# A decoder trunk whose sixteen head pairs each get an ending of their own: parts or whole product last, and another token order in the next matmuls

## The chip, the core and the metric

The kernel runs on one core of one Trainium2 chip. The metric is device time in microseconds (us) of one execution; the time before is the median of three runs, 2437.17 us (2436.08 to 2437.2). Lower is better.

## What is computed

A causal decoder trunk of two layers over 256 tokens with 2048 features, 16 heads of 128, and a gated MLP of 5632. Cut to what matters:

```python
for i in range(DEPTH):                      # DEPTH = 2
    a = rmsnorm(h, attn_norm[i])
    if i % 2 == 0:   # 8 stick-breaking heads, then 8 dilated-window heads
        h = h + sb_dilated_mixer(a, positions, w_in_even[i // 2], w_out_even[i // 2])
    else:            # 16 forgetting-attention heads
        h = h + fox_mixer(a, w_in_odd[i // 2], b_forget[i // 2], w_out_odd[i // 2])
    h = h + conv_ffn(rmsnorm(h, ffn_norm[i]), w_up[i], conv_w[i], conv_b[i], w_down[i])
    gate = jax.nn.sigmoid(rmsnorm(h, ple_norm[i]) @ w_ple_gate[i])
    h = h + gate * (p[i] @ w_ple[i])
return rmsnorm(h, final_norm)
```

Every head computes scores from q and k, a weighting of them, and the product of these weights with v.

## The kernel before, in words

Activations lie feature by token (128 partitions by 256 tokens). Each operand of a projection is split into a high part, rounded to the matmul type F32R, and a low part, the rest; a product is three matmuls, `PARTS = ((0, 0), (0, 1), (1, 0))`: high by high, high by low, low by high. Weights are streamed by DMA (`issue_group`, L160) and split by ScalarE and VectorE (L176, L177) into a ring of four tiles `w`. Almost all of TensorE's work is of one shape: a stationary 128x128 tile and 256 moving columns. `gemm_unit` (L222 to L232) issues 24 such matmuls for four blocks of the contraction, `gemm_v` (L258 to L267) the same with the roles of weight and activation exchanged, and each such unit ends with one `tick`. Tile names: `psq`, `psk`, `psv` are the projections to q, k and v, `psp` the per-layer embedding, `pso` the projection out of the mixer, `psu`, `psd`, `psg` the MLP up, down and the gate.

Two heads are worked on at a time. Pair number = 8 times the layer + the pair in its layer: pairs 0 to 3 are stick-breaking, 4 to 7 dilated, 8 to 15 forgetting heads. A pair's attention is put into the stream of projection matmuls as three short pieces, by `defer(n, fn)`, which runs `fn` after n more ticks, so that VectorE and ScalarE have the time of some units for the softmax:

- the scores (`sb_first` L467 or `sm_first` L511, tile `scs`): per head one product of whole float32 operands q and k (128x128), and three matmuls of parts with 256 columns. In `sm_first` the whole product stands ahead of the parts; forgetting heads have a third product ahead of both (L518);
- the second piece: for stick-breaking pairs the suffix sums (`sb_second` L492, F32R throughout), for the others six float32 transposes (`sm_second` L553, L559), tile `sps`;
- the product with the values (`attend` L575, tile `avp`): per head one whole float32 product (L580) and three of parts (L583), the whole one ahead.

So in a trace every piece ends either with **parts last** (F32R) or with **float32 last**, and the projection goes on behind it. All is one in-order stream on TensorE; nothing but the program's order decides what stands there.

Behind every piece `shake()` sets a count of two. The next two matmuls of `gemm_unit` or `gemm_v` then go through their 256 tokens (in `gemm_v` columns) in another order, on the moving side and in PSUM alike, so that the result is the same:

```python
def walk(ap):
    return ap.rearrange("p (a b c) -> p b a c", a=2, c=8)
```

Eight tokens of the first half, eight of the second, and so on. This is called a walk of side 8 over two matmuls, (8, 2), below. Three more shakes stand outside the pairs: five and eight ticks after the start of the first layer's projections, and behind the forget gates at the start of the second layer. Other pieces on TensorE have no shake behind them: the sums of a norm (`norm_sums` L321, tile `nps`), its rows (`norm_rows` L337, `rps`), both float32, and the running sums of the forget gates (`cps`, L612 to L620, float32).

Of the kernel before, what the change touches and what calls it, by code (L numbers as in the profile page):

```python
# [17 lines left out]
P = 128  # L18
D = 2048
S = 256  # L20
# [80 lines left out]
GROUPS = _groups(UNITS)  # L101


@with_exitstack
def trunk(ctx: ExitStack, tc: tile.TileContext, xT, pT, pos, gains, conv, bf, cst, wst, out):
    nc = tc.nc
# [30 lines left out]
    def at_tile(name):  # L137
        return psum.tile([P, 2, 512], F32, name=name, tag="at", bufs=2)
# [6 lines left out]


    raws, ready = [], []
    at = {"group": 0, "off": 0, "unit": 0, "tick": 0, "rows": 0, "shake": 0}

    def issue_group():  # L150
        g = GROUPS[at["group"]]
# [42 lines left out]
    def defer(n, fn):  # L194
        later.append((at["tick"] + n, fn))
# [10 lines left out]
    PARTS = ((0, 0), (0, 1), (1, 0))  # L206
# [1 line left out]


    def walk(ap):  # L210
        return ap.rearrange("p (a b c) -> p b a c", a=2, c=8)

    def shake():
        at["shake"] = 2

    def walks(*aps):
        if not at["shake"]:
# [290 lines left out]

    SEG = ((0, 128), (128, 384))

    def sm_first(q, k, prepared, fox):  # L511
        full, one = prepared
        sc = at_tile("scs")
        for j in range(2):
            if fox is not None:
                c2, sel, cq, h0 = fox
                lh = sel[:, h0 + j:h0 + j + 1].to_broadcast([P, P])
                nc.tensor.matmul(sc[:, j, 0:384], lhsT=lh, rhs=c2, start=True, stop=False,  # L518
                                 skip_group_check=True)
            nc.tensor.matmul(sc[:, j, 0:128], lhsT=q[:, j, 0:128], rhs=k[:, j, 0:128],  # L520
                             start=fox is None, stop=True, skip_group_check=True)
            for n, (a, b) in enumerate(PARTS):
                nc.tensor.matmul(sc[:, j, 128:384], lhsT=one[a][:, j, :], rhs=full[b][:, j, :],  # L523
                                 start=False, stop=n == 2, skip_group_check=True)
        shake()
        s, pe = t3_tile("s", (P, 2, 384)), t3_tile("pe", (P, 2, 384))
        if fox is None:
            msk = ct[:, C_MDL:C_MDL + 384].unsqueeze(1).to_broadcast([P, 2, 384])
            nc.vector.tensor_add(out=s, in0=sc[:, :, :384], in1=msk)
        else:  # L530
            for j in range(2):
                for t, (a, b) in enumerate(SEG):
                    nc.vector.scalar_tensor_tensor(
                        out=s[:, j, a:b], in0=sc[:, j, a:b], scalar=cq[:, t, h0 + j:h0 + j + 1],
                        in1=ct[:, C_MFX + a:C_MFX + b], op0=ALU.add, op1=ALU.add)
        mx = work.tile([P, 2, 2], F32, name="mx", tag="mx", bufs=2)
        sm = work.tile([P, 2, 2], F32, name="sm", tag="sm", bufs=2)
        rsm = work.tile([P, 2, 2], F32, name="rsm", tag="rsm", bufs=2)
        for t, (a, b) in enumerate(SEG):
            nc.vector.tensor_reduce(out=mx[:, t, :], in_=s[:, :, a:b], axis=AX.X, op=ALU.max,  # L540
                                    negate=True)
        for j in range(2):
            for t, (a, b) in enumerate(SEG):
                nc.scalar.activation(out=pe[:, j, a:b], in_=s[:, j, a:b], func=AF.Exp,
                                     bias=mx[:, t, j:j + 1], accum_out=sm[:, t, j:j + 1])
        nc.vector.reciprocal(out=rsm, in_=sm)
        for t, (a, b) in enumerate(SEG):
            for j in range(2):
                nc.vector.tensor_scalar_mul(out=pe[:, j, a:b], in0=pe[:, j, a:b],
                                            scalar1=rsm[:, t, j:j + 1])  # L550
        return pe, s

    def sm_second(pe, s):  # L553

        sp = at_tile("sps")
        for j in range(2):
            for i in range(3):
                o = sp[:, 0, j * S + i * P:j * S + (i + 1) * P] if i < 2 else sp[:, 1, j * P:(j + 1) * P]
                nc.tensor.transpose(out=o, in_=pe[:, j, i * P:(i + 1) * P], identity=ident)  # L559
        shake()  # L560
        w = in_parts(sp[:, 0, :].rearrange("p (j s) -> p j s", j=2), "w")
        w1 = s.rearrange("p a b -> p (a b)")[:, 0:256]
        nc.scalar.copy(out=w1, in_=sp[:, 1, 0:256])
        return w, w1
# [7 lines left out]
        else:  # L572
            nc.scalar.activation(out=v[1], in_=ps, func=AF.Copy, scale=rT[:, 1:2])

    def attend(hp, w, v, dst):  # L575
        w, w1 = w
        av = at_tile("avp")
        for j in range(2):
            js = slice(j * P, (j + 1) * P)
            nc.tensor.matmul(av[:, 0, j * S + 128:(j + 1) * S], lhsT=v[1][:, js], rhs=w1[:, j * P:(j + 1) * P],  # L580
                             start=j == 0, stop=False, skip_group_check=True)
            for n, (a, b) in enumerate(PARTS):
                nc.tensor.matmul(av[:, 0, j * S:(j + 1) * S], lhsT=v[0][:, a, js], rhs=w[b][:, j, :],  # L583
                                 start=False, stop=n == 2, skip_group_check=True)
        shake()
        parts(dst[:, 2 * hp:2 * hp + 2], av[:, 0, :].rearrange("p (j s) -> p j s", j=2))


# [42 lines left out]
    def head_pair(l, hp, act, dst, st):  # L631
        q = work.tile([P, 2, S], F32, name="q", tag="qkv", bufs=2)
        k = work.tile([P, 2, S], F32, name="k", tag="qkv", bufs=2)
        v = (work.tile([P, 2, S], F32R, name="vp", tag="vp"), work.tile([P, S], F32, name="v", tag="v"))
        full = _cuts(KT)
        if l % 2 == 1 and hp == 0:
            ps = at_tile("psv")
            gemm_vf(ps, act, l)
            for t in range(2):
                values(v, t, ps[:, t, 0:S])  # L640
            st["fox"] = forget_gates(l, ps)
            shake()
        ps = mm_tile("psq")
        gemm(ps, act, "w_in", l, hp * 256, full)
        with_rows(lambda ps=ps: nc.vector.tensor_mul(out=q, in0=ps, in1=rq2))
        ps = mm_tile("psk")
        gemm(ps, act, "w_in", l, D + hp * 256, full)
        with_rows(lambda ps=ps: nc.vector.tensor_mul(out=k, in0=ps, in1=rb2))
        late = max(0, at["rows"] - at["tick"])

        def first():
            if l % 2 == 0 and hp < 4:
                a = sb_first(q, k, st["parts"])
                defer(5, lambda: second(lambda: sb_second(*a)))
            else:
                a = sm_first(q, k, st["parts"], st["fox"] + (2 * hp,) if l % 2 == 1 else None)
                defer(4, lambda: second(lambda: sm_second(*a)))

        def second(fn):
            w = fn()  # L660
            defer(2, lambda: attend(hp, w, v, dst))

        if l % 2 == 0 and hp >= 4:
            rope(q)
            rope(k)

        def prepare():

            if l % 2 == 0 and hp < 4:
                st["parts"] = in_parts(q, "f"), tile_parts(k[:, :, 0:128])  # L670
            else:
                st["parts"] = in_parts(k, "f"), tile_parts(q[:, :, 128:256])

        with_rows(prepare)

        defer(late + (2 + (l % 2 == 0 and hp >= 4) if hp == 7 or (l % 2 == 1 and hp == 0) else 4), first)
        if l % 2 == 1 and hp == 0:
            return
        ps = mm_tile("psv")
        gemm_v(ps, act, l, 2 * D + hp * 256)  # L680
        for i in range(2):
            values(v, i, ps[:, i, :])
# [29 lines left out]
    for l in range(DEPTH):  # L712
        st = {}
        if l == 0:
            split_unit()
            rest_of_start()

            for op in range(8):
                if op in (3, 5, 7):
                    norm_parts(op // 2 - 1, 0, X, tc.keep_in_program_order)  # L720
                ple_up(0, op)
            norm_parts(3, 0, X, tc.keep_in_program_order)
            for i in range(4, 8):
                defer(1 + (i > 5), lambda i=i: norm_parts(i, 0, X, tc.keep_in_program_order))
            constants()
            for i in range(8):
                defer(3 + i, lambda i=i: norm_squares(i, tc.keep_in_program_order))
            norm_finish(True, 12, 14)
            for n in (5, 8):
                defer(n, shake)  # L730
        for hp in range(NH // 2):
            head_pair(l, hp, X, Y, st)
            if l > 0:
# [34 lines left out]
        for op in range(8):  # L768
# [21 lines left out]
            else:  # L790
                more = []
                for j in range(2):
                    for k in range(KT):
                        for n, (a, b) in enumerate(((0, 0), (0, 1), (1, 0))):
                            nc.tensor.matmul(ps[j],  # L795
                                             lhsT=ws[k // 4][:, k % 4, a, j * P:(j + 1) * P],
                                             rhs=X[:, k, b, :], start=k == 0 and n == 0,
# [99 lines left out]
```

## Time and profile before

| | |
|---|---|
| median of three runs | 2437.17 us |
| the profiled execution, its own time | 2434.39 us |
| its span (first to last instruction) | 2432.2 us |
| TensorE matmuls (PE) | 2416.6 us busy, 99%, 21056 records |
| TensorE weight loads (PEld) | 2414.8 us busy, 99% |
| VectorE, ScalarE | 1613.5 us (66%), 1246.2 us (51%) |
| granted TensorE clock | 0.998 |
| TensorE's idle time that a wait explains | 7.1 us in four waits |

A span of PE is pipelined, so "busy" does not say how fast matmuls follow each other. That is read from the chain of waits: a row there gives a start, a duration and a count (`x96`), and duration by count is the time from one matmul to the next. A float32 matmul is recorded as two (`x4` for two instructions).

### The profile page before, as it was taken

What the parts mean: (1) busy time and instruction counts of PE and PEld (TensorE: products, weight loads), DVE (VectorE), ACT (ScalarE), POOL (GpSimd) and SP (SyncE); (2) the same over time, 40 slices, a digit from 0 to 9 for tenths busy, and PEclk for the clock granted to TensorE, in tenths of its full rate; (3) what the DMA queues carried; (4) which work ended last, traced back from release to release, by engine and by line L of the source; (5) the groups of instructions that cost most, each with busy time, mean ns of one, the idle gap of its engine ahead of it and who ended that gap; (6) DMA issues with size and microseconds to landing.
All of it is one profiled execution on the core that took longest, in us unless ns stands there. A gap on an engine that the chain in (4) does not pass through costs nothing.

```text
span 2432.2 us, 48172 instructions
## 1 busy us (share of the span) xinstructions
PE 2416.6 (99%) x21056; PEld 2414.8 (99%) x21056; DVE 1613.5 (66%) x2130; ACT 1246.2 (51%) x1594; POOL 5.9 (0%) x13
## 2 busy tenths in 40 slices
PE   9999999999999999999999999999999999999998
PEld 9999999999999999999999999999999999999997
DVE  7767766776567657767766565666765766577666
ACT  6654455554355445555554454555543554455554
POOL 0000000000000000000000000000000000000000
PEclk9999999999999999999999999999999999999999
DMA  7444455555555555555555454555555555555553
GB/s 281 164 179 167 172 181 183 193 196 198 193 191 192 187 205 197 192 182 204 178 186 176 170 176 160 192 189 191 193 197 197 193 191 185 200 198 194 183 204 122
DMA packets 66818, 458.05 MB, mean 188 GB/s; under 512 B 7552, under 2 KB 7840, under 8 KB 16944
## 3 DMA queue, kind: packets, MB, share of 16 engines
q1 hardware_dynamic: 66576, 454.93, 52.5%
q8 instruction: 164, 2.69, 0.4%
q14 instruction: 46, 0.38, 0.0%
q0 software_dynamic: 32, 0.06, 0.0%
HBM read 452.86 MB, written 2.10 MB: 187 GB/s over the span
## 4 chain that ended last, share of the span: by engine, by line
PE 98%; DMA 1%; DVE 1%; SPq 0%; issue 0%; ACT 0%; POOLq 0%; DVEq 0%
PE psu L232 39%; PE psd L232 20%; PE pso L232 7%; PE psk L232 7%; PE psv L267 7%; PE psq L232 7%; PE psg L232 7%; PE psv L280 0%; PE avp L583 0%; PE psp L232 0%; PE pse L795 0%; DMA h<-in_x 0%; PE scs L523 0%; DMA cv<-in_conv 0%; PE sps L559 0%; PE avp L580 0%
## 5 line engine op out<-in xcount | busy, mean ns | idle before, releaser
L177 DVE TENSOR_TENSOR w<-wr,w 128x1024 fp32r<-128x1024 f32 (+2 forms) x874 | 1046.2, 1197 | 664.7 <-ACT w L176 662.6
L176 ACT CAST w<-wr 128x1024 fp32r<-128x1024 f32 (+2 forms) x874 | 900.6, 1031 | 1041.0 <-PE psu L232 355.0
L232 PE MATMUL psu<-act,w 128*128 128x256 f32 x8448 | 960.3, 276 | 0.0
L232 PEld LDWEIGHTS psu<-act,w 128*128 128x128 f32 x8448 | 959.0, 188 | 0.1
L232 PE MATMUL psd<-act,w 128*128 128x256 f32 x4224 | 479.7, 276 | 0.0
L232 PEld LDWEIGHTS psd<-act,w 128*128 128x128 f32 x4224 | 479.2, 188 | 0.0
L232 PE MATMUL psq<-act,w 128*128 128x256 f32 x1536 | 182.7, 279 | 2.8 <-DVE act L301 2.8
L232 PE MATMUL psk<-act,w 128*128 128x256 f32 x1536 | 184.5, 280 | 0.0
L232 PEld LDWEIGHTS psq<-act,w 128*128 128x128 f32 x1536 | 179.1, 188 | 3.3 <-DVE act L301 3.0
L232 PEld LDWEIGHTS psk<-act,w 128*128 128x128 f32 x1536 | 181.3, 189 | 0.1
L232 PE MATMUL pso<-act,w 128*128 128x256 f32 x1536 | 181.3, 281 | 0.0
L232 PEld LDWEIGHTS pso<-act,w 128*128 128x128 f32 x1536 | 180.6, 189 | 0.0
L267 PE MATMUL psv<-w,act 128*128 128x256 f32 x1440 | 172.3, 279 | 0.0
L267 PEld LDWEIGHTS psv<-w,act 128*128 128x128 f32 x1440 | 170.7, 188 | 0.0
L232 PE MATMUL psg<-act,w 128*128 128x256 f32 x1440 | 164.8, 276 | 0.0
L232 PEld LDWEIGHTS psg<-act,w 128*128 128x128 f32 x1440 | 163.9, 188 | 0.1
L691 DVE TENSOR_TENSOR u<-psu,rb 128x512 f32<-128x512 f32 x88 | 60.8, 691 | 33.0 <-PE psu L232 32.8
L697 DVE SCALAR_TENSOR_TENSOR yv<-u,cv,yv 128x256 f32<-128x256 f32 x176 | 73.3, 477 | 0.0
L697 DVE SCALAR_TENSOR_TENSOR yg<-u,cv,yg 128x256 f32<-128x256 f32 x176 | 73.3, 477 | 0.0
L694 ACT ACTIVATE yg<-u,cv 128x256 f32<-128x256 f32 x88 | 48.1, 593 | 1.1 <-DVE u L691 1.1
L694 ACT ACTIVATE yv<-u,cv 128x256 f32<-128x256 f32 x88 | 48.0, 593 | 0.0
L291 ACT CAST act<-yg 128x512 fp32r<-128x512 f32 x44 | 27.4, 622 | 39.3 <-DVE yg L707 39.3
(182 smaller groups left out, 969.7 us busy)
## 6 DMA issues: line engine op xcount, KB each, us to landing
wr<-in_w SPq DMA_DIRECT2D x388, 1024.0 KB, 4.8
wr<-in_w SPq DMA_DIRECT2D x36, 768.0 KB, 4.3
wr<-in_w SPq DMA_DIRECT2D x8, 896.0 KB, 4.6
h<-in_x SPq DMA_DIRECT2D x4, 512.0 KB, 8.5
wr<-in_w SPq DMA_DIRECT2D x4, 512.0 KB, 10.2
out_dram<-h SPq DMA_DIRECT2D x7, 256.0 KB, 2.5
wr<-in_w SPq DMA_DIRECT2D x2, 816.0 KB, 4.4
pl<-in_w SPq DMA_DIRECT2D x3, 512.0 KB, 7.1
```

Of the source, the lines that this page charges most:

```text
L176: nc.scalar.copy(out=w[:, :, 0, :], in_=raw)
L177: nc.vector.tensor_sub(out=w[:, :, 1, :], in0=raw, in1=w[:, :, 0, :].bitcast(F32))
L232: nc.tensor.matmul(to, lhsT=w[:, k, s, j * P:(j + 1) * P], rhs=rows, start=first and i == 0, stop=last and k == kc - 1 and n == 2, skip_gr ...
L267: nc.tensor.matmul(to, lhsT=act[:, 4 * i + k, a, tsl], rhs=cols, start=i + t + k + n == 0, stop=i == 3 and k == kc - 1 and n == 2, skip_gr ...
L291: nc.scalar.copy(out=dst[:, :, 0, :], in_=src)
L691: nc.vector.tensor_mul(out=u[:, :, 2:], in0=ps, in1=rb2)
L694: nc.scalar.activation(out=y[:, j, :], in_=u[:, j, 2:], func=AF.Identity, bias=cv[:, l, t, 3:4], scale=cv[:, l, t, 2:3])
L697: nc.vector.scalar_tensor_tensor(out=y[:, j, :], in0=u[:, j, tap:tap + S], scalar=cv[:, l, t, tap:tap + 1], in1=y[:, j, :], op0=ALU.mult, ...
```

## The change

Nothing but the order inside three kinds of pieces and the walks behind them changes. On VectorE, ScalarE, GpSimd and SyncE the order of instructions is the same as before, and TensorE executes the same number of matmuls of the same shapes.

`walk` takes its side from a variable, and `shake` takes a way (side, count), with (0, 0), no walk, where none is given. So the ends of `sb_first` and `sb_second` and the place behind the forget gates, whose `shake()` is untouched, now have no walk. `sm_first` and `attend` take a kind, "p" for parts last (as before) or "w" for the whole float32 product last. The tables `SCORES`, `TURNS` and `VALUES` give each pair its ways:

| pair | scores | transposes | product with v |
|---|---|---|---|
| 0 | no walk | no walk | w (8, 2) |
| 1 | no walk | no walk | w, no walk |
| 2 | no walk | no walk | p (4, 1) |
| 3 | no walk | no walk | w (16, 2) |
| 4 | w, no walk | (8, 2) | p (8, 1) |
| 5 | w (8, 1) | (8, 1) | w (4, 1) |
| 6 | w (8, 2) | (4, 1) | w (4, 2) |
| 7 | p (4, 1) | (16, 2) | p (16, 1) |
| 8 | w (16, 2) | (8, 2) | w, no walk |
| 9 | p (16, 2) | (8, 2) | w (8, 1) |
| 10 | p (4, 1) | (8, 1) | w (8, 2) |
| 11 | p (4, 2) | (8, 1) | w (16, 2) |
| 12 | p (32, 2) | (16, 2) | p (16, 2) |
| 13 | w, no walk | (4, 1) | p (4, 1) |
| 14 | w (8, 1) | (4, 2) | p (4, 2) |
| 15 | w (8, 2) | no walk | p (32, 2) |

(For pairs 0 to 3 "transposes" stands for the suffix sums.) Of the two shakes at the start one is left, (4, 1).

```diff
+WAYS = (("w", 0, 0), ("w", 8, 1), ("w", 8, 2), ("w", 16, 2), ("p", 16, 2), ("p", 4, 1), ("p", 4, 2), ("p", 32, 2))
...
     def walk(ap):
-        return ap.rearrange("p (a b c) -> p b a c", a=2, c=8)
-
-    def shake():
-        at["shake"] = 2
+        return ap.rearrange("p (a b c) -> p b a c", a=2, c=at["side"])
+
+    def shake(way=(0, 0)):
+        at["side"], at["shake"] = way
...
+            if kind == "p":
+                whole()
             for n, (a, b) in enumerate(PARTS):
                 nc.tensor.matmul(sc[:, j, 128:384], lhsT=one[a][:, j, :], rhs=full[b][:, j, :],
-                                 start=False, stop=n == 2, skip_group_check=True)
-        shake()
+                                 start=fox is None and kind == "w" and n == 0, stop=n == 2, skip_group_check=True)
+            if kind == "w":
+                whole()
+        shake(way)
...
-        shake()
+        shake(TURNS[pair])
...
+            todo = [(av[:, 0, j * S + 128:(j + 1) * S], v[1][:, js], w1[:, j * P:(j + 1) * P])]
+            inp = [(av[:, 0, j * S:(j + 1) * S], v[0][:, a, js], w[b][:, j, :]) for a, b in PARTS]
+            todo = todo + inp if kind == "p" else inp + todo
+            for n, (o, x, y) in enumerate(todo):
+                nc.tensor.matmul(o, lhsT=x, rhs=y, start=j + n == 0, stop=n == 3, skip_group_check=True)
+        shake(way)
...
-            for n in (5, 8):
-                defer(n, shake)
+            defer(5, lambda: shake((4, 1)))
```

Three places show what this does to TensorE's stream. First the product with the values of pair 9 and the projection behind it, before (`s,v` is the whole product, `wh` and `wl` are the parts; a size written `128x16x2x8` is a walk of side 8):

```order
L580 MATMUL avp<-s,v 128x128
L583 MATMUL avp<-wh,vp 128x256
L583 MATMUL avp<-wl,vp 128x256
L583 MATMUL avp<-wh,vp 128x256
L580 MATMUL avp<-s,v 128x128
L583 MATMUL avp<-wh,vp 128x256
L583 MATMUL avp<-wl,vp 128x256
L583 MATMUL avp<-wh,vp 128x256
L232 MATMUL psk<-act_71,w 128x16x2x8 x2
L232 MATMUL psk<-act_71,w 128x256 x70
```

and after the change:

```order
L604 MATMUL avp<-wh,vp 128x256
L604 MATMUL avp<-wl,vp 128x256
L604 MATMUL avp<-wh,vp 128x256
L604 MATMUL avp<-s,v 128x128
L604 MATMUL avp<-wh,vp 128x256
L604 MATMUL avp<-wl,vp 128x256
L604 MATMUL avp<-wh,vp 128x256
L604 MATMUL avp<-s,v 128x128
L243 MATMUL psk<-act_71,w 128x16x2x8
L243 MATMUL psk<-act_71,w 128x256 x71
```

The float32 product has moved to the end of each head, and one matmul walks where two did. Second, the same piece of pair 7, the last of its layer, with the long projection behind it; before, from its second head on:

```order
L580 MATMUL avp<-s,v 128x128
L583 MATMUL avp<-wh,vp 128x256
L583 MATMUL avp<-wl,vp 128x256
L583 MATMUL avp<-wh,vp 128x256
L232 MATMUL pso<-act_71,w 128x16x2x8 x2
L232 MATMUL pso<-act_71,w 128x256 x646
```

and after:

```order
L604 MATMUL avp<-s,v 128x128
L604 MATMUL avp<-wh,vp 128x256
L604 MATMUL avp<-wl,vp 128x256
L604 MATMUL avp<-wh,vp 128x256
L243 MATMUL pso<-act_71,w 128x8x2x16
L243 MATMUL pso<-act_71,w 128x256 x647
```

Here the order stays, and one walk of side 16 takes the place of two of side 8. Third, the end of the scores of stick-breaking pair 2, before:

```order
L475 MATMUL scs<-fl,xp 128x256
L475 MATMUL scs<-fh,xp 128x256 x2
L475 MATMUL scs<-fl,xp 128x256
L475 MATMUL scs<-fh,xp 128x256
L232 MATMUL psq<-act_70,w 128x16x2x8 x2
L232 MATMUL psq<-act_70,w 128x256 x94
```

and after:

```order
L486 MATMUL scs<-fl,xp 128x256
L486 MATMUL scs<-fh,xp 128x256 x2
L486 MATMUL scs<-fl,xp 128x256
L486 MATMUL scs<-fh,xp 128x256
L243 MATMUL psq<-act_70,w 128x256 x96
```

The walk is gone, and the projection's first 96 matmuls are all plain.

More of the change, by code (lines that the diff above doesn't have):

```diff
@@ L101 @@
 GROUPS = _groups(UNITS)
+WAYS = (("w", 0, 0), ("w", 8, 1), ("w", 8, 2), ("w", 16, 2), ("p", 16, 2), ("p", 4, 1), ("p", 4, 2), ("p", 32, 2))
+SCORES = {4: ("w", 0, 0), 5: ("w", 8, 1), 6: ("w", 8, 2), 7: ("p", 4, 1),
+          **{8 + i: WAYS[(i + 3) % 8] for i in range(8)}}
+TURNS = {4: (8, 2), 5: (8, 1), 6: (4, 1), 7: (16, 2), 8: (8, 2), 9: (8, 2), 10: (8, 1), 11: (8, 1),
+         12: (16, 2), 13: (4, 1), 14: (4, 2), 15: (0, 0)}
+VALUES = {0: ("w", 8, 2), 1: ("w", 0, 0), 2: ("p", 4, 1), 3: ("w", 16, 2), 4: ("p", 8, 1), 5: ("w", 4, 1),
+          6: ("w", 4, 2), 7: ("p", 16, 1), **{8 + i: WAYS[i] for i in range(8)}}
 @with_exitstack
@@ L147, in trunk @@
     raws, ready = [], []
-    at = {"group": 0, "off": 0, "unit": 0, "tick": 0, "rows": 0, "shake": 0}
+    at = {"group": 0, "off": 0, "unit": 0, "tick": 0, "rows": 0, "shake": 0, "side": 8}
     def issue_group():
@@ L509, in trunk, with sm_first @@
     SEG = ((0, 128), (128, 384))
-    def sm_first(q, k, prepared, fox):
+    def sm_first(pair, q, k, prepared, fox):
         full, one = prepared
+        kind, *way = SCORES[pair]
         sc = at_tile("scs")
@@ L519, in sm_first, with whole @@
                                  skip_group_check=True)
-            nc.tensor.matmul(sc[:, j, 0:128], lhsT=q[:, j, 0:128], rhs=k[:, j, 0:128],
-                             start=fox is None, stop=True, skip_group_check=True)
+            def whole():
+                nc.tensor.matmul(sc[:, j, 0:128], lhsT=q[:, j, 0:128], rhs=k[:, j, 0:128],
+                                 start=fox is None and kind == "p", stop=True, skip_group_check=True)
+            if kind == "p":
+                whole()
             for n, (a, b) in enumerate(PARTS):
                 nc.tensor.matmul(sc[:, j, 128:384], lhsT=one[a][:, j, :], rhs=full[b][:, j, :],
-                                 start=False, stop=n == 2, skip_group_check=True)
-        shake()
+                                 start=fox is None and kind == "w" and n == 0, stop=n == 2, skip_group_check=True)
+            if kind == "w":
+                whole()
+        shake(way)
         s, pe = t3_tile("s", (P, 2, 384)), t3_tile("pe", (P, 2, 384))
@@ L551, in sm_first, with sm_second @@
         return pe, s
-    def sm_second(pe, s):
+    def sm_second(pair, pe, s):
         sp = at_tile("sps")
@@ L573, in values, with attend @@
             nc.scalar.activation(out=v[1], in_=ps, func=AF.Copy, scale=rT[:, 1:2])
-    def attend(hp, w, v, dst):
+    def attend(pair, w, v, dst):
         w, w1 = w
+        hp = pair % 8
+        kind, *way = VALUES[pair]
         av = at_tile("avp")
@@ L579, in attend @@
             js = slice(j * P, (j + 1) * P)
[L580 to L585, printed above, removed]
+            todo = [(av[:, 0, j * S + 128:(j + 1) * S], v[1][:, js], w1[:, j * P:(j + 1) * P])]
[4 more added lines that the diff above has]
+        shake(way)
         parts(dst[:, 2 * hp:2 * hp + 2], av[:, 0, :].rearrange("p (j s) -> p j s", j=2))
@@ L655, in first @@
             else:
-                a = sm_first(q, k, st["parts"], st["fox"] + (2 * hp,) if l % 2 == 1 else None)
-                defer(4, lambda: second(lambda: sm_second(*a)))
+                a = sm_first(8 * l + hp, q, k, st["parts"], st["fox"] + (2 * hp,) if l % 2 == 1 else None)
+                defer(4, lambda: second(lambda: sm_second(8 * l + hp, *a)))
         def second(fn):
             w = fn()
-            defer(2, lambda: attend(hp, w, v, dst))
+            defer(2, lambda: attend(8 * l + hp, w, v, dst))
         if l % 2 == 0 and hp >= 4:
```

## The prediction

> **What bounds the kernel now.** I read the page first, then the waits of TensorE, then the chain of waits in order of time, stretch by stretch. On the page:
>
> ```profile
> PE 2416.6 (99%) x21056; PEld 2414.8 (99%) x21056; DVE 1613.5 (66%) x2130; ACT 1246.2 (51%) x1594; POOL 5.9 (0%) x13
> ...
> PEclk9999999999999999999999999999999999999999
> ```
>
> TensorE is busy from end to end at a full clock, and the next engine has a third of its time free. Nothing but TensorE's own pace can matter, unless it is made to wait; the waits show four, all at the start or the end:
>
> ```profile
> PE psq L232 <- DVE act L301: 2.8, 1, 2.8
> PE nps L321 <- DVE sq L806: 1.6, 1, 1.6
> PE rps L337 <- ACT nd L336: 1.5, 1, 1.5
> PE idle L382 <- DVE act L379: 1.2, 1, 1.2
> ```
>
> So the question is how fast one matmul of 256 columns follows another. The chain of waits (start, duration, what, count) gives it by stretch, here from the last value product of the first layer into the MLP:
>
> ```profile
> 328.64 76.33 PE pso L232 x648
> 404.98 8.48 PE psu L232 x72
> 413.79 5.57 PE psu L232 x48
> 419.36 0.43 PE rps L337 x2
> 419.79 160.49 PE psu L232 x1416
> ...
> 667.33 152.32 PE psu L232 x1344
> ```
>
> There are two paces. 152.32 / 1344 is 113.33 ns; 76.33 / 648 is 117.79 ns, and the 72 matmuls behind, of another projection, keep that pace (8.48 / 72 = 117.8). It ends when norm sums (a float32 piece of 0.4 us between 413.46 and 413.79) pass through: the 48 behind them take 5.57, 116.0 each with the restart in it, and the 1416 after the norm rows 160.49 / 1416 = 113.34. The windows show the same without any chain, equal stretches of 70 us at a granted clock of 1.00 with 620 and 597 matmuls:
>
> ```profile
> 670.00:740.00 70.00, 70.00 (x620) 70.00 (x619) 48.87 (x68) 37.01 (x44) 0.00 (x0) 1.00 0.54 196
> 330.00:400.00 70.00, 70.00 (x597) 70.00 (x596) 43.74 (x52) 35.10 (x46) 0.00 (x0) 1.00 0.53 189
> ```
>
> VectorE and ScalarE do less in the window with 597, so they do not explain it. I call them the 113 pace and the 118 pace. A pace belongs to TensorE's stream: a piece of attention leaves one or the other behind, and it then lasts until the next piece. A matmul at the 118 pace costs 117.79 - 113.33 = 4.46 ns, taken as 4.45. The whole change comes down to how many matmuls go at each pace.
>
> **What each ending leaves behind today.** All walks are (8, 2). Behind products with the values, parts last:
>
> ```profile
> 95.39 8.49 PE psq L232 x72
> 103.88 2.83 PE psk L232 x24
> 114.27 2.84 PE psk L232 x24
> 117.11 11.31 PE psv L267 x96
> ...
> 1496.54 8.49 PE psk L232 x72
> 1505.03 5.66 PE psv L267 x48
> ...
> 1529.23 81.98 PE pso L232 x696
> 1611.21 8.48 PE psu L232 x72
> ```
>
> Every one of these is at 117.8 to 118.3: 16 endings of 16 leave the 118 pace. They hold 96 matmuls (pair 0), 120 (pairs 1, 2, 3, 6, 8, 14), 144 (4, 5), 168 (9 to 13), and the two long ones, 648 + 72 = 720 (pair 7) and 696 + 72 = 768 (pair 15): 3432 in all, 15.3 us.
>
> Behind scores, parts last too, for a stick-breaking, a dilated and two forgetting pairs:
>
> ```profile
> 129.58 10.92 PE psq L232 x96
> ...
> 202.62 11.32 PE psq L232 x96
> ...
> 1254.70 8.49 PE psq L232 x72
> ...
> 1290.35 8.17 PE psq L232 x72
> ```
>
> The 113 pace behind stick-breaking scores (113.8, four of four), the 118 pace behind dilated ones (117.9, four of four), and behind forgetting scores the 113 pace six times (113.5, pairs 9 to 14) and the 118 pace twice (117.9, pairs 8 and 15). Behind the transposes, float32 last:
>
> ```profile
> 214.59 5.48 PE psk L232 x48
> ...
> 251.32 5.67 PE psk L232 x48
> ```
>
> Ten of twelve are like the first (114.2, the 113 pace), pairs 5 and 6 like the second (118.1). Norm sums and norm rows, float32 last with no walk, left the 113 pace all ten times where 256-column matmuls followed; the forget gates' running sums, float32 too, did not:
>
> ```profile
> 1234.31 0.43 PE cps L620 x2
> 1234.75 2.83 PE psq L232 x24
> 1237.57 11.31 PE psk L232 x96
> ```
>
> So float32 last is followed by the 113 pace in 20 of 23 cases. Parts last has one answer for each kind of piece, and for values that is always the 118 pace.
>
> **The change part by part.** Edits with one answer first. TensorE's count and shapes stay. Turning from float32 to F32R costs a longer step, and both orders turn as often:
>
> ```profile
> 327.33 0.38 PE L580 MATMUL avp<-s,v 128*128 128x128 f32 x2
> 327.47 0.36 PE L583 MATMUL avp<-wh,vp 128*128 128x256 f32 x1
> 327.67 0.28 PE L583 MATMUL avp<-wl,vp 128*128 128x256 f32 x1
> 327.79 0.28 PE L583 MATMUL avp<-wh,vp 128*128 128x256 f32 x1
> ```
>
> The step at the turn is 0.20 us (327.47 to 327.67) against 0.12 at the next. Two heads turn twice either way; with float32 last the second turn merely falls on the projection: nothing. Walked matmuls go from 102 to 56. Their price is at most the difference between 24 matmuls with two walks (2.84, at 114.27) and 24 without (2.83, at 103.88), 5 ns each, so the 46 fewer are worth 0 to 0.2 us; I take nothing. New waits: with float32 last the value product needs the split weights first and `w1` last, the other way round than today. Two units of projection lie between their making and their use (2 x 24 matmuls, over 5.4 us at the 113 pace) and hide either. Without that cover TensorE would stand before a ScalarE copy, with the projections queued behind it, for at most what a ScalarE cast of a larger tile takes:
>
> ```profile
> L176 ACT CAST w<-wr 128x1024 fp32r<-128x1024 f32 (+2 forms) x874 | 900.6, 1031 | 1041.0 <-PE psu L232 355.0
> ```
>
> 1.03 us a pair, 16.5 us for sixteen. I take nothing, since no such wait exists today. Now the terms that count, each a number of matmuls times 4.45 ns times the share that changes pace.
>
> 1. Values with float32 last (pairs 0, 1, 3, 5, 6, 8 to 11): 96 + 3 x 120 + 144 + 120 + 3 x 168 = 1224 matmuls, all at the 118 pace today. Bounds: none changes (16 of 16 today) or all do (norm sums). The nearest row is the transposes', but of the four that came out of a 118 stretch only two left the 113 pace, so I take a share of 0.7: 857 matmuls, -3.8 us.
> 2. Values with parts last and another walk (2, 4, 7, 12 to 15): 2208 matmuls, of which 1488 in the two long ones. Bounds 0 (today) to 0.8 (scores of forgetting pairs). I take 0.35: 773, -3.4 us, about the price of one long stretch.
> 3. Scores with float32 last that leave the 118 pace today (pairs 4, 5, 6, 8, half of 15): 4 x 96 + 48 = 432, share 0.7: -1.35 us.
> 4. Scores that leave the 113 pace today and change: pairs 9 to 12 (parts last, other walks), 4 x 84, share lost 0.4; pairs 13, 14 (float32 last), 168, share lost 0.3: 184 matmuls, +0.8 us.
> 5. Stick-breaking scores and sums lose their walks: 384 + 144 = 528 matmuls at the 113 pace today. No row shows a parts-last ending without a walk. Bounds: none lost, or all lost (+2.35 us); I take half, +1.2 us.
> 6. Transposes: seven of the ten that leave the 113 pace get another walk or none (336 matmuls, a fifth lost), the other two (96) change with 0.7: 67 against 67, nothing.
> 7. The start: the first projections have 70 matmuls at the 113 pace and then 96 at the 118 pace today, the second walk standing between them:
>
> ```profile
> 32.17 11.03 PE psk L232 x96
> 43.20 11.31 PE psv L267 x96
> ```
>
> With one walk of side 4 I take half of both; and half of the 72 behind the forget gates, now at the 113 pace, is lost: together +0.1 us.
>
> Sum: -3.8 - 3.4 - 1.35 + 0.8 + 1.2 + 0.1 = -6.4 us. The profiled execution would go from 2434.39 to 2428.0. It lies 2.8 us under the median of the runs, so the forecast for the median is 2437.17 - 6.4 = 2430.8.
>
> [...]
>
> **The rivals.** What a measurement of this kernel can tell from no change is about 0.2%, 4.9 us, or 1095 matmuls net.
>
> - *Parts last never lets go of the 118 pace behind values* (0.27). For it: 16 of 16. Against: other pieces with parts last do. Term 2 falls away: -3.0 us, 2434.1.
> - *The endings reset nearly everywhere, both long stretches included* (0.15). For it: the ten norm pieces. 0.8 x 3432 x 4.45 ns is 12.2 us, with terms 3 to 7 (+0.75) -11.4, 2425.7.
> - *The pace does not hang on the endings at all, or what is won is lost elsewhere* (0.10): a piece's place, not its order and walk, sets the pace, and the change doesn't do what it says; 2437.2. For it: pairs 4 and 5 end their transposes alike and leave different paces. [...] Against: the same places give one answer per kind of piece.
> - *The lost and altered walks let the 113 stretches fall* (0.06). The place is the first matmuls behind scores, sums and transposes. At the 113 pace today are 384 + 144 + 504 + 480 = 1512 matmuls there; if all fall while values stay at 118, it is 6.7 us slower, 2443.9. It decides from 1095 matmuls lost net.
> - The forecast has 0.42: mixed results, at 4.5 to 9 us won, 2428 to 2432.7.
>
> **How the numbers follow.** Faster by over 0.2%: 0.36 of the forecast's 0.42 (its lower part falls short of 4.9), 0.03 of the first rival, 0.15 of the second: 0.54. Slower: 0.05 of the last. Within: 0.41. The range goes from the second rival, 2425.5, to 2436.5, just short of no change; outside lie most of the third rival (0.07), the last (0.06), and the lower half of the second (0.07), 0.2 together.
>
> **What would show it.** Right: in the chain of the changed kernel the rows behind float32-last value products at 113.3 to 114.5 in six or more of nine; one of the two long `pso` stretches at 113.3 (73.4 us for 648, or 78.9 for 696) or neither; granted clock as before; no new wait on PE. Wrong: all value stretches at 117.8; 113 rows of today, such as `psq` behind stick-breaking scores at 10.92 for 96, now at 11.3 in most places; a PE wait ahead of `avp`; or 597 matmuls in every window of 70 us.

## The result and the profile after

The changed kernel takes 2423.57 us in the median of four runs (2422.55 to 2425.64), against 2436.62 for the kernel before beside it: 13.05 us less, ratio 0.9948 (95% interval 0.9930 to 0.9965). It is faster by 0.5%, by twice the forecast of 6.4 us, and lies 1.9 us below the low end of the range.

The profiled execution took 2424.25 us with a span of 2422.5. The two long stretches in the chain of waits (start, duration, what, count):

```profile
327.45 73.46 PE pso L243 x648
400.91 8.17 PE psu L243 x72
...
1522.88 78.91 PE pso L243 x696
1601.79 8.17 PE psu L243 x72
```

Both go at the 113 pace (73.46 / 648 = 113.4, 78.91 / 696 = 113.4, and 8.17 / 72 = 113.5 behind each). The same window that held 597 matmuls now holds 620, at the same granted clock and with VectorE a little busier:

```profile
330.00:400.00 70.00, 70.00 (x620) 70.00 (x619) 45.15 (x53) 36.75 (x47) 0.00 (x0) 1.00 0.52 185
```

Behind the shorter value products, from the chain again: pair 0, pair 1 (two rows), pair 3 and pair 12 in this order (each row is of the stretch behind the product).

```profile
97.82 8.20 PE psq L243 x72
...
116.29 2.83 PE psk L243 x24
119.12 11.31 PE psv L278 x96
...
191.96 10.88 PE psv L278 x96
...
1422.36 11.30 PE psv L278 x96
```

Pairs 0 and 3 left the 113 pace (8.20 / 72 = 113.9, 10.88 / 96 = 113.3), pairs 1 and 12 the 118 pace as before. In all, 11 of the 16 value products now leave the 113 pace. Elsewhere:

```profile
131.59 10.88 PE psq L243 x96
...
203.98 10.90 PE psq L243 x96
...
251.24 5.66 PE psk L243 x48
...
275.56 11.32 PE psq L243 x96
...
320.63 5.66 PE pso L243 x48
...
1220.85 8.48 PE psq L243 x72
...
1230.65 2.75 PE psq L243 x24
1233.40 10.89 PE psk L243 x96
...
1436.58 8.48 PE psq L243 x72
```

Read from the top: stick-breaking scores without a walk keep the 113 pace and need no run-up (10.88 against 10.92); dilated scores have turned at pair 4, not at pair 6; transposes have lost the 113 pace at pairs 5 and 7; the projection behind the forget gates has lost it (8.48 against 8.20), and the 156 matmuls behind the running sums have won it (10.89 against 11.31 for the 96 of them in `psk`), which no term of the forecast held; scores of pair 13 have lost it.

The running sums are a case to remember: neither kernel has a walk behind them, and nothing in that piece changed. Entered from a projection at 113 (8.20 for 72, before) they left 118; entered at 118 (8.48) they left 113. e1 and e4 below repeat the first, e2, e3, e6, m1 and m2 the second. And a pace can also turn with no piece between. Behind the scores of pair 7 the 24 matmuls of `psv` go at 118 and the 72 of `pso` right behind them at 113.6, here as before the change and in every run below; why, no trace shows:

```profile
308.97 2.83 PE psv L278 x24
311.80 8.18 PE pso L243 x72
```

A count over all stretches of the chain from the first norm sums on says it in one number: 4164 matmuls of 256 columns went at the 118 pace before, 1332 now. 2832 x 4.45 ns is 12.6 us. The start of this execution was late by 2.5 us (the first `psv` starts at 45.71, 43.20 before), which is why its own time shows 10.1 us of the 13.05.

### The profile page after: what moved, and what is told of

Same layout as the page of the kernel before. It is cut to its first block, busy times and chain, and to the rows that moved or that the text cites. A ratio compares the mean times of both kernels' runs of the same rounds, so it can differ in the third digit from the quotient of the medians.

```text
span 2422.5 us, 48169 instructions
## 1 busy us (share of the span) xinstructions
PE 2405.5 (99%) x21056; PEld 2402.7 (99%) x21056; DVE 1613.6 (67%) x2130; ACT 1247.0 (51%) x1594; POOL 5.8 (0%) x13
## 4 chain that ended last, share of the span: by engine, by line
PE 98%; DMA 1%; DVE 0%; ACT 0%; SPq 0%; issue 0%; POOLq 0%; DVEq 0%
PE psu L243 40%; PE psd L243 20%; PE psk L243 7%; PE pso L243 7%; PE psq L243 7%; PE psv L278 7%; PE psg L243 7%; PE avp L604 1%; DMA wr<-in_w 1%; PE psv L291 0%; PE pse L814 0%; PE psp L243 0%; PE scs L539 0%; PE sps L577 0%; DMA h<-in_x 0%; PE scs L533 0%
## 5 line engine op out<-in xcount | busy, mean ns | idle before, releaser
L243 PE MATMUL pso<-act,w 128*128 128x256 f32 x1536 | 175.5, 276 | 0.0
L243 PEld LDWEIGHTS pso<-act,w 128*128 128x128 f32 x1536 | 174.8, 188 | 0.0
```

What stands on the lines that cost most here:

```text
L243: nc.tensor.matmul(to, lhsT=w[:, k, s, j * P:(j + 1) * P], rhs=rows, start=first and i == 0, stop=last and k == kc - 1 and n == 2, skip_gr ...
```

## The experiments

The theory, A: each ending has its own answer, 113 or 118, set by the kind of piece, the order in it and the walk behind it. The rivals: B, that a pair's place in the program decides; C, that float32 last does it, whatever walks. All runs are compared with the kernel before on the same chip. The edits are given in short, as what each pair then gets, not as the lines themselves. "Entered at" a pace means that the stretch just ahead of the piece goes at that pace.

| run | time us | ratio to before (95%) | matmuls at 118 | of them behind values |
|---|---|---|---|---|
| before (beside the runs) | 2436.62 to 2437.89 | | 4164 | 3432 |
| changed | 2423.57 | 0.9948 (0.9930 to 0.9965) | 1332 | 696 |
| e1, long walks alone | 2430.44 | 0.9970 (0.9960 to 0.9981) | 2676 | 1944 |
| e2, parts last, no walk | 2436.94 | 1.0000 (0.9990 to 1.0009) | 4440 | 3432 |
| e3, float32 last, no walk | 2435.79 | 0.9996 (0.9986 to 1.0006) | 4140 | 3432 |
| e4, float32 last, (8, 2) | 2423.51 | 0.9944 (0.9927 to 0.9961) | 900 | 264 |
| e5, best of each | 2418.73 | 0.9923 (0.9911 to 0.9935) | 192 | 0 |
| e6, walks kept, parts last | 2429.03 | 0.9967 (0.9955 to 0.9979) | 2328 | 1512 |
| m1, reads alone | 2423.44, one run | | 1332 | 696 |
| m2, writes alone | 2436.07, one run | | 3900 | 3432 |
| e7, more walks | 2426.01, one run | | 1860 | 1392 |

**Two walks and nothing else (e1).** The kernel before with

```diff
-VALUES 7: ("p", 8, 2)    15: ("p", 8, 2)
+VALUES 7: ("p", 16, 1)   15: ("p", 32, 2)
```

> The kernel before, with one edit: the walk behind the value products of pairs 7 and 15 is (16, 1) and (32, 2), as in the changed kernel; every other ending as before. Theory A (each ending has its own answer, set by the kind of piece, the order in it and the walk behind it, wherever it stands): both pso stretches and the 72 psu matmuls behind each go at 113.3 ns, nothing else moves, -3.2 and -3.4 us, 2430.0. Theory B (what went before, the pair's place or the earlier stretches, sets the pace): both stay at 117.8, 2436.6. Theory C (float32 last does it): no float32-last value product here, 2436.6.

Measured 2430.44, 6.6 us less than before, as A has it. The two rows in its chain:

```profile
331.69 73.46 PE pso L239 x648
...
1529.09 78.91 PE pso L239 x696
```

From the first norm sums on, all other stretches have the durations of before to within 0.02 us. Half of the change's gain comes from which way two walks go, without any matmul moved; C is out as the sole cause (there is no float32-last value product here), and B for these two places.

**The order alone, both ways, without walks (e2, e3).**

```
e2: ("p", 0, 0) in all scores and values, (0, 0) behind all transposes, no shake at the start
e3: ("w", 0, 0) in all scores and values, the rest as in e2
```

> The order of before everywhere (parts last), and no walk anywhere. Theory A: stick-breaking pieces stay at 113.3 as in the changed kernel; transposes without walk 113.3 in all twelve (one case known), values unknown, taken as 117.8; forgetting scores unknown. Between 2432 (forgetting scores keep 113.3) and 2439 (they fall). Theory C (order alone): as before, 2436.6. A rival within A, that the walk of side 8 over two matmuls is itself what holds the values at 117.8: values at 113.3, 2421 or less.

> Float32 last in all value products and all dilated and forgetting scores, and no walk anywhere. Theory A: values at 117.8 (as pairs 1 and 8 of the changed kernel), dilated scores 113.3 (as pair 4), forgetting scores 117.8 (as pair 13), transposes 113.3: about +0.5 us on before, 2437. Theory C (float32 last does it): all values at 113.3, 2419 to 2421.

Both are within 0.1% of before. All 16 value products leave the 118 pace in either order, the long ones among them; first e2, then e3:

```profile
330.46 76.32 PE pso L239 x648
...
1532.07 81.97 PE pso L239 x696
```

```profile
330.07 76.32 PE pso L239 x648
...
1532.27 81.98 PE pso L239 x696
```

So float32 last by itself does nothing for values (C falls), and the walk (8, 2) of before was not what held them at 118 (the rival in e2's expectation falls). The same runs show that transposes without any walk leave the 113 pace twelve times of twelve, in both. One place went against e2's expectation: the suffix sums of pair 1, entered at 118, leave 118 (5.66 for 48), though they leave 113 in e3 and in e6 from the same entry and with no walk either.

**Float32 last with the old walk (e4).**

```diff
-kind, *way = VALUES[pair]      (SCORES likewise)
+kind, way = "w", (8, 2)        (and (8, 2) at every other place, as before)
```

> Float32 last in all value products and all dilated and forgetting scores, with the walk (8, 2) of before behind every piece. Theory A: all sixteen value stretches at 113.3 (as pairs 0 and 10 of the changed kernel), dilated scores 117.8 (as pair 6), 3432 matmuls times 4.45 ns = -15.3 us, about 2421.5, less if forgetting scores fall as well (to 2423.7). Theory B (place): a mixture, 2424 to 2436.

Measured 2423.51. 14 of 16 value products turn; pairs 5 and 6 do not. What the chain shows apart at these two is the pace ahead of the piece: pair 4 is entered at 113 (5.48, the first row) and leaves `psv` at 10.88, pair 5 is entered at 118 (5.67 at 251.07) and leaves it at 11.31:

```profile
214.94 5.48 PE psk L239 x48
...
221.59 5.49 PE psk L239 x48
227.07 10.88 PE psv L274 x96
...
251.07 5.67 PE psk L239 x48
257.89 5.67 PE psk L239 x48
263.56 11.31 PE psv L274 x96
```

Theory A has to be widened: the pace on entry can matter too. That entry is the cause at pairs 5 and 6 is argued, not shown: pair 10 of the changed kernel is entered at 118 with the same ending and turned.

**The walks kept, the order undone (e6).**

```diff
-kind, *way = VALUES[pair]      (SCORES likewise)
+kind, way = "p", VALUES[pair][1:]
```

> The changed kernel's walks, but parts last in every value product and score, as before. Theory A (order and walk together): with float32 last undone, values of pairs 0, 3, 5, 10, 11 go back to 117.8, 9 and 6 stay at 113.3, 1 and 8 stay at 117.8, some scores fall: +3 to +4 us on the changed kernel, about 2427. If the walk alone decides: as the changed kernel, 2423.6. If float32 last alone decides: all value stretches at 117.8 but those of pairs 4, 7, 14, 15.

Measured 2429.03, 5.5 us over the changed kernel by the medians (the kernel before beside it was 0.8 us later too), 996 matmuls more at 118 (4.4 us). Values of pairs 0, 3, 5, 10 and 11 go back, 1, 8, 2, 12, 13 stay as they were, 9 keeps the 113 pace, all as expected; pair 6, (4, 2), was expected to keep it and did not. Pairs 9 and 10:

```profile
1302.16 8.19 PE psk L239 x72
1310.35 10.88 PE psv L274 x96
...
1339.76 8.49 PE psk L239 x72
1348.25 11.31 PE psv L274 x96
```

So neither the walk nor the order decides alone; for most walks it is the two together. Over all runs but m2, value products with float32 last leave 113 in 30 of 32 cases with a walk behind them, of five kinds, and in none of 20 without; with parts last it depends on the walk, and without one it is none of 18.

Scores did not follow so simply. Those of pair 9 have the same ending, parts last with (16, 2), and are entered at 118 in both kernels, yet the 72 matmuls behind them take 8.17 in the changed kernel and 8.48 here, with `psv` ahead in the first row of each:

```profile
1271.37 11.31 PE psv L278 x96
...
1285.56 8.17 PE psq L243 x72
```

```profile
1272.16 11.30 PE psv L274 x96
...
1286.38 8.48 PE psq L239 x72
```

What differs nearest ahead is the order in the pieces of pair 8. So an ending and the pace on entry are not all that counts; the rival by which what went before matters still stands for scores.

**Which side of the walk acts (m1, m2).** A walk goes through tokens in another order on both sides, reads in SBUF and writes in PSUM. Each kernel has one of them alone, and so doesn't compute the trunk:

```diff
-        return [walk(x) for x in aps]
+m1:     return [aps[0].rearrange("p (b a c) -> p b a c", a=2, c=c), walk(aps[1])]
+m2:     return [walk(aps[0]), aps[1].rearrange("p (b a c) -> p b a c", a=2, c=c)]
```

> The changed kernel, but in the walked matmuls only the moving operand in SBUF is read in the other order and PSUM is written straight, so that these matmuls add to other tokens than they should. If the order of the SBUF reads is what acts: every stretch as in the changed kernel, about 2423.6, pso stretches at 113.3. If the PSUM writes act: as without walks, both pso stretches at 117.8, float32-last values at 117.8, about 2436.

> The changed kernel, but in the walked matmuls only the PSUM writes go in the other order and the moving operand is read straight, so that these matmuls add to other tokens than they should. If the order of the PSUM writes is what acts: as the changed kernel, about 2423.6. If the reads act: as without walks, about 2436, both pso stretches at 117.8.

The rows of the long stretches, of m1 and then of m2:

```profile
326.11 73.46 PE pso L240 x648
...
1521.52 78.91 PE pso L240 x696
```

```profile
329.74 76.32 PE pso L240 x648
...
1530.40 81.97 PE pso L240 x696
```

With the reads alone every stretch from the first norm sums on has the pace that it has in the changed kernel, 1332 matmuls at 118 in both, and the time is 2423.44. With the writes alone all value products are at 118 and the time is 2436.07. So the order in which TensorE reads the moving operand of one or two matmuls gives the whole effect, and behind values the order of the PSUM writes gives none of it. The writes cost nothing either: 76.32 with a walk of side 16 in the writes, 76.32 with no walk at all in e2, and 2.83 for the 24 matmuls behind the values of pair 2 in both, with a walk of side 4 and without. The Trainium skill (PSUM — Partial Sum Buffer, Specifications) says that any non-contiguous access pattern in PSUM slows matmuls significantly; for these runs of 16 bytes and more no row here shows it.

Behind scores m2 leaves a question. Forgetting scores of pairs 9 to 12, parts last and entered at 118, leave 113 in m2, while those of pairs 9 to 14 all leave 118 in e2, with no walk at all. For pair 9, m2 and then e2:

```profile
1276.80 11.31 PE psv L275 x96
...
1290.97 8.17 PE psq L240 x72
```

```profile
1277.25 11.30 PE psv L274 x96
...
1291.46 8.48 PE psq L239 x72
```

Either the walked writes act there, or the order in the pieces ahead does, float32 last in m2 and parts last in e2, as between the changed kernel and e6 above. No run separates the two.

**The best known ending everywhere (e5).** Its tables, with two more walks at the start of the second layer:

```diff
+values: 0 w (8, 2); 1 to 6 and 8 to 14 p (8, 1); 7 p (16, 1); 15 p (32, 2)
+scores: 4 to 6 w; 7, 8 p; 9 to 14 p (16, 2); 15 p (16, 1); no walk where none is named
+transposes and stick-breaking pieces: no walk
-            defer(5, lambda: shake((4, 1)))
+            defer(5, lambda: shake((8, 2)))
...
+            shake((8, 2))        # behind the forget gates
+            shake((8, 1))        # behind their running sums
```

> Each ending gets the way that left 113 ns in an earlier run: values of pairs 1 to 6 and 8 to 14 parts last with one walk of side 8 (known from pair 4 alone), pair 0 float32 last (8, 2), 7 and 15 as in the changed kernel; dilated scores 4 to 6 float32 last without walk; forgetting scores parts last, none for pair 8, (16, 2) for 9 to 14, (16, 1) for 15; no walk behind transposes, stick-breaking pieces and scores 7; (8, 2) at the start and behind the forget gates, and one new walk (8, 1) behind the gates' running sums. Theory A: all but some 300 of the 4232 matmuls that are at 117.8 in the kernel before go at 113.3, -17.5 us, about 2419. Theory B (place): the pairs that get pair 4's ending do not follow it, 13 stretches with 1824 matmuls stay slow, about 2427.

Measured 2418.73 (2416.73 to 2418.86), ratio 0.9923 (0.9911 to 0.9935): faster than the kernel before, 4.8 us under the median of the changed kernel, and what A says to 0.3 us. One ending known from pair 4 alone when this was planned, parts last with (8, 1), leaves the 113 pace at all 13 places that got it, all entered at 113. Windows behind both long products:

```profile
330.00:400.00 70.00, 70.00 (x620) 70.00 (x620) 46.14 (x54) 37.74 (x50) 0.00 (x0) 1.00 0.55 196
1530.00:1600.00 70.00, 70.00 (x620) 70.00 (x619) 46.50 (x56) 36.70 (x47) 0.00 (x0) 1.00 0.53 192
```

One surprise: the scores of pair 8, parts last without a walk and entered at 113, leave 118 here and left 113 in e2 from the same entry.

**More walks at known places (e7).** e5 with

```diff
+values: 1 (32, 1); 2 (64, 1); 3 (64, 2); 4 (16, 3); 5 (8, 3); 6 (4, 3); 8 (8, 2);
+        9 (16, 1); 10 (16, 2); 11 (32, 2); 12 (4, 2); 13 (32, 1); 14 (64, 1)
```

> The kernel of the fifth run, with other walks behind the parts-last value products. Known ways at new places: theory A says 113.3 ns for (16, 1) at pair 9, (32, 2) at pair 11, (4, 2) at pair 12, and 117.8 for (8, 2) at pair 8 and (16, 2) at pair 10; theory B (place) says all five stay at 113.3, as these places were in the fifth run. New ways: (32, 1) at pairs 1 and 13 and (64, 1) at pairs 2 and 14 give the same answer at both places by theory A; (64, 2), (16, 3), (8, 3), (4, 3) at pairs 3 to 6 are open. Time 2418.7 + 288 x 4.45 ns = 2420.0 if all new ways give 113.3, 2424.0 if none does.

Measured 2426.01, later than either expectation, since scores fell as well: at pairs 4, 5 and 11, now entered at 118 (276 matmuls). Those of pairs 6, 9, 13 and 14, entered at 118 as well, kept the 113 pace. Pairs 9 to 12:

```profile
1309.77 10.88 PE psv L274 x96
...
1347.45 11.30 PE psv L274 x96
...
1385.61 10.88 PE psv L274 x96
...
1423.32 11.31 PE psv L274 x96
```

(16, 1) and (32, 2) hold, (8, 2) and (16, 2) fail as they did elsewhere: four of the five carry to new places, and the two that fail speak against B, by which these places would have stayed at 113. (4, 2) fails at pair 12, entered at 113; it succeeded at pair 14 of the changed kernel and of e6, entered at 118, and failed at pair 6 of e6, entered at 113. That fits the widened theory. (32, 1) and (64, 1) leave 118 at both their places, (64, 2), (16, 3) and (8, 3) leave it too, (4, 3) leaves 113. With parts last there is no order in it by side or by count: one walk of side 8 works and two or three do not, two of side 32 work and one does not.

What stays open is the mechanism inside TensorE: what the reads run into, and why the later pace then holds for 768 matmuls. Nothing in a trace shows the reads themselves.

## Why the prediction was wrong

**What bounds the kernel, and the unit of account: right.** Two paces of 113.3 and 117.8 ns, held in almost all places from one piece to the next (not behind the scores of pair 7, nor, in most runs, of pair 15), 4.45 ns a matmul. The time worked out from the count of matmuls at 118 and the kernel before beside it fits every run of the table to 1.7 us.

**Edits costed at nothing: right.** No new wait of weight on PE (five new rows of waits, 1.3 us in all, none over 0.3); the turn between float32 and F32R falls on the projection's first matmul with float32 last, and e3, with float32 last everywhere and no walk, differs from e2 by 1.2 us, about what their counts at 118 say (300 matmuls, 1.3 us).

**Term 1, values with float32 last, share 0.7 (857 matmuls): right in size, by luck.** 984 of 1224, -4.4 us against -3.8; seven of nine places, where six or more were said. The rows that it went by, transposes and norm sums with float32 last, did not carry: e3 shows that without a walk float32 last brings the 113 pace nowhere behind values. It takes a walk with it.

**Term 2, values with parts last and another walk, "I take 0.35: 773, -3.4 us, about the price of one long stretch": the step that failed.** 1752 of 2208 turned, share 0.79, -7.8 us, both long stretches among them (e1 has them alone: -6.6). So one walk of side 16 or two of side 32 are enough to turn a stretch behind parts last, and m1 shows that it is their reads that do it. The share was taken nearest to the 16 of 16 of today, as though these were sixteen draws. They were one: the same ending, (8, 2), sixteen times, which gives one answer. They said nothing about other walks.

**Term 3, dilated and forgetting scores with float32 last: right in size.** 288 of 432, -1.3 us against -1.35.

**Term 4, scores that leave the 113 pace today: too dear.** Only pair 13 fell, 84 matmuls, +0.4 against +0.8.

**Term 5, "stick-breaking scores and sums lose their walks; I take half, +1.2 us": wrong.** None of the 528 was lost. They keep the 113 pace without a walk (one exception in e2), and the run-up behind a walk is saved (10.92 to 10.88; over the eight endings 0.3 us).

**Term 6, transposes, nothing: too cheap.** Five of the seven changed ones fell and one of the other two turned, 192 matmuls, +0.85 us. Without a walk, as e2 and e3 show, none would have.

**Term 7, the start, +0.1: right by accident.** The first projections and the 72 behind the forget gates went to 118, and the 156 behind the running sums, not in the sum, to 113: about nothing together.

The measured terms are -4.4 - 7.8 - 1.3 + 0.4 - 0.3 + 0.85 = -12.55 us, with term 7 at nothing; the forecast had -6.4. Of the 6 us between, 4.4 are term 2 and 1.5 term 5; the others nearly cancel.

**The rivals.** The nearest was the second, "reset nearly everywhere, both long stretches included", with 0.15 and 2425.7: 2736 of 3432 value matmuls turned, its 0.8. Its mechanism is not what happened (norm pieces tell nothing of values), its size is. The range ended at its middle, and so outside the result: a range that is to hold a case must reach to the case's own far side. The first rival, that parts last never lets go behind values, and the third, that the pace does not hang on the endings at all, are refuted by e1: the same matmuls in the same order, four of them at most with another order of tokens, and 6.6 us. The chance of 0.54 for faster was too low for the same reason as term 2.

## What to carry to other kernels

Where TensorE is busy from end to end, divide a chain row's duration by its count: two values for one shape mean that something ahead of the stretch set its pace. The slower stretches have up to 4% to give without moving work (4.46 of 117.79 ns), which was 0.5% of this kernel's time in the change and 0.8% in e5. Try the ending of the piece ahead of the longest stretch first, since one walked matmul in place of two was worth 3.2 us behind pair 7 (2.87 in `pso`, 0.31 in `psu`); try several ways, since no rule by size told which works, and check each where it will stand, with the pieces ahead as they will be. And count repeated equal cases as one observation, not as many.

## What the runs showed of the hardware

- Matmuls of 256 columns with a weight load each follow each other at 113.33 or at 117.79 ns at a granted clock of 1.00. They kept the later pace for up to 768 matmuls, the earlier one for 6288 (before, from the norm rows at 419.36 to the next norm sums). The Trainium skill (TensorE: Matmul & The Clock Gate, Back-to-back issue gap) gives N / 2.4 + 2.5 ns as the gap of an isolated warm matmul, 109.2 ns for 256 columns by estimate, and says that in a stream of weight loads and matmuls both operations set the spacing. Neither pace here is 109.2.
- Reading the moving operand of one or two matmuls in another order changes which pace follows (m1: `pso` 73.46 for 648). Writing PSUM in another order does not, behind values (m2: 76.32), and cost nothing there: 76.32 for 648 with runs of 16 float32 and with none, 2.83 for 24 with runs of four and with none. Behind forgetting scores it is open whether the writes act.
- The answers repeat behind values: the same order, walk and entry gave the same pace in all runs but one case, float32 last with (8, 2) entered at 118 (113 at pair 10 of the changed kernel, 118 at pairs 5 and 6 of e4).
- Behind the other pieces they repeat less. With the same ending and entry, different paces were left by the scores of pair 8 (e2 against e5), those of pair 9 (changed kernel against e6), dilated scores with float32 last and no walk (pair 4: e3 against e7), the suffix sums of pair 1 (e2 against e3), and, in the kernel before, the transposes of pairs 4 and 5 and the forgetting scores of pairs 8 and 9. Place, or more of what went before than its pace, matters there.
